# Weights traced two blocks ahead, and norms in a fixed TensorE order, in a two-block transformer kernel

## The chip, the cores and the metric

The kernel runs on one core of one Trainium2 chip. The metric is the device time of one execution in microseconds (us). The engines are named as in the profile: PE is TensorE (PEld its weight loads), DVE is VectorE, ACT is ScalarE, POOL is GpSimd, SP is SyncE, which issues the loads of the weights.

## The reference, cut to what matters

The input is 256 tokens of 1024 channels, in fp32. A first block has four layers of attention (differential, latent, dilated, differential) with a SwiGLU each, all with rms norms. The second block, cut to its core, is where most of the change lies; the dilated attention of the first block (layer C) is the other place.

```
def second_block(x, ...):
    h = layer_norm(x, ln_in_g, ln_in_b)
    for l in range(2):
        mix = token_mix(h, ...)
        h = layer_norm(DEEPNORM_ALPHA * h + mix, ln1_g[l], ln1_b[l])
        ffn = conv_ffn(h, w_up[l], ffn_dw_w[l], ffn_dw_b[l], w_down[l])
        h = layer_norm(DEEPNORM_ALPHA * h + ffn, ln2_g[l], ln2_b[l])
    return h

def token_mix(h, ...):
    z = h @ w_in + b_in
    u_pool, u_conv, q, k, v, qi, ki, wi, gates = split_cols(z, IN_SIZES)
    ...                                  # rope on q, k, qi, ki
    y_pool = pool_mixer(u_pool, pool_w, pool_scale) @ w_pool_out
    y_conv = conformer_conv(u_conv, ...) @ ...       # glu, 31 taps, layer norm, silu
    y_attn = dsa_attention(q, k, v, qi, ki, wi) @ w_attn_out
    g = jax.nn.sigmoid(gates).reshape(B, L, 3, D_MODEL)
    return (g[:, :, 0] * y_pool + g[:, :, 1] * y_conv + g[:, :, 2] * y_attn) @ w_o

def conv_ffn(h, w_up, ffn_dw_w, ffn_dw_b, w_down):
    u = causal_dwconv(h @ w_up, ffn_dw_w, ffn_dw_b)  # 3 taps
    gate, val = jnp.split(u, 2, axis=-1)
    return (jax.nn.silu(gate) * val) @ w_down
```

In `dsa_attention` an index score (8 heads, relu, weighted sum) selects the 64 best keys of each query, and the attention of 8 heads with 2 key heads runs over these.

## The kernel before

Activations lie transposed: `self.x[k]` is a chunk of 128 channels by 256 tokens, k from 0 to 7. Every large product is made of three (`mm3`): operands are split into a high and a low part, and high by high, high by low and low by high are summed in PSUM.

`weights` (L295) brings one block of weights: two pieces of up to 1024 columns; for each a load on SP's queue (L303), the high part `whi` by ScalarE (`act`, L236) and the low part `wlo` by VectorE (L308). There are five buffers for raw pieces and six for split ones, so three blocks of two pieces fit in the split buffers.

The order of each engine is written when the kernel is built: of the instructions that are ready, the one that comes first in the trace (the order in which the Python code makes them) goes first. Only where `self.woven` is set are products and transposes (`matmul` L264, `transpose` L318) held on TensorE in the order of the trace. In such stretches (layer C and `token_mix`) short steps are put between the products of the projections: `later(delay, step)` puts a step into a heap with a due time, `tick(us)` moves a planned clock forward by an estimate after each product, and due steps are traced then.

In `token_mix` the products of the projections come in this order: w_zqi (index queries), w_zb (keys, values), w_zq (queries), w_zs 0 (pool), w_zs 1 and 2 (glu of the convolution), then ten gate blocks (w_zs 5 to 14, j from 2 to 11 in the loop) with two blocks of convolution taps (w_tap) after j = 3 and j = 5. Woven in as steps are: `turn` (transposes of the roped qi and q), `keys`, `index` (one head of the index score), `greatest` (a round of the top-k on VectorE: two max and two replace operations), `roped`, `tapped` (three convolution taps on VectorE), `pooled`, and `attend`, `returned`, `mixed` (the attention). The rounds of the top-k are due 1.5 apart, the steps of attend 6.0 apart.

`deepnorm` adds a residual chunk by chunk as the products of a projection end; per chunk `seen` makes the square, sums x on VectorE and the square on GpSimd (`moments`, k 0 to 6 added, the last one left over), and splits x times the gain for early products. `entry` does the same at the start of the second block, with a third sum `st["x"]`. `normed` then calls `stats` (`compact` sums over channels with one-column matmuls against `onesd`, L1055; `spread` makes the scale and the shift on VectorE and GpSimd and broadcasts them by transposes, L319), makes the products of two weight blocks with the not yet normalised x (k 0 to 7, so the norm is applied to their results), and `ln_apply` normalises x itself for the blocks that follow. `self.woven` is not set there. The last norm has its own `last_norm`, which calls `compact` too.

Of the kernel before, what the change touches and what calls it, by code (L numbers as in the profile page):

```python
# [14 lines left out]
AF = mybir.ActivationFunctionType  # L15
# [196 lines left out]
class Program:  # L212
# [82 lines left out]
    def weights(self, ap, unit, eng=None):  # L295
# [52 lines left out]
    def mmode(self, aps, n, kb, xs):  # L348
        ps = [self.mm_bank()[:, :n] for _ in range(2)]
        for b, ap in enumerate(aps):  # L350
            w = self.ready.pop() if self.ready else self.weights(ap, n)
            kt = [(k, t) for k in range(kb) for t in range(2)]
            if b == len(aps) - 1:
                kt.sort(key=lambda a: a[1])
            for k, t in kt:
                kk = b * kb + k
                xh, xl = xs[kk]
                tk = slice(t * 128, t * 128 + 128)
                self.mm3(ps[t], (xh[:, tk], xl[:, tk]), w(k, 0, n),
                         b == 0 and k == 0, b == len(aps) - 1 and k == kb - 1)  # L360
                if self.woven:
                    self.tick(3 * US[n])
        return ps
# [191 lines left out]
    def project(self, w, xs, consume, late=None, eng=None):  # L555

        for j in range(4):
            wt = self.weights(w[j], 256, eng)
# [305 lines left out]
    def dilated(self, l, own):  # L864
# [18 lines left out]
        self.woven = True  # L883
        v, done = {}, [0]

        def values(hq):
            for g in range(3):
                v[hq // 2, g] = self.v_block([wv[g, hq], wv[g, hq + 1]], xs, r)

        def queries(hq):  # L890
# [4 lines left out]
            for g in (1, 2, 0):  # L895
                ps = self.mmode([wqk[g, hq][0], wqk[g, hq][1]], 512, 4, xs)
                toks = list(self.qk_tokens(ps, r, "ropeC", -0.125))
# [93 lines left out]
        for j in range(4):  # L991
            wt[j] = self.weights(self.ins["w_co"][j], 256)
# [44 lines left out]

    def moments(self, k, chunk, accs, eng):

        if k == 0:  # L1040
            accs.append(self.wk.tile([128, 256], F32, name="acc", tag="acc", bufs=3))
            eng.tensor_copy(accs[0], chunk)
        elif k < 7:
            eng.tensor_add(accs[0], accs[0], chunk)  # L1044
        else:
            accs.append(chunk)

    def compact(self, sums):
# [3 lines left out]
        for r in range(m):  # L1052
            for n, a in enumerate(sums):
                for t in range(2):
                    self.nc.tensor.matmul(ps[:, 2 * n + t:2 * n + t + 1], a[r][:, t * 128:(t + 1) * 128],  # L1055
                                          self.onesd[:, 0:1], start=r == 0 and n == 0 and t == 0,
                                          stop=r == m - 1 and n == len(sums) - 1 and t == 1,
                                          skip_group_check=True)
        return ps
# [11 lines left out]
    def spread(self, mean, sq, eps, extra=None):  # L1071
# [19 lines left out]
        self.stt(b, m, -1.0, r, OP.mult, OP.mult)  # L1091
        return self.bcast(r, b)

# [56 lines left out]
    def seen(self, st, k):  # L1150
        x = self.x[k]
        sq = self.t1("sq")
        self.act(sq, x, AF.Square)
        self.moments(k, x, st["m"], self.nc.vector)
        self.moments(k, sq, st["q"], self.nc.gpsimd)
        if st["early"]:
# [138 lines left out]
    def token_mix(self, l, st):  # L1295
# [21 lines left out]

        def by_token(w, o):

            bz = bias(o, 512)  # L1320
            ps = self.mmode([w[l, 0], w[l, 1]], 512, 4, xs)
            tok = [self.t2("qtok") for _ in range(2)]
# [12 lines left out]
        qiT = self.slot()  # L1335
        for t, q in enumerate(by_token(i["w_zqi"], 0)):
            self.rope(heads(q, 8), 8, 32, *tab[t])
# [3 lines left out]
        bz = bias(512, 328)  # L1341
        ps = self.mmode([i["w_zb"][l, 0], i["w_zb"][l, 1]], 328, 4, xs)
        kd = self.t2("zkd", (2, 256))
# [32 lines left out]
        def index(hh):  # L1376
# [11 lines left out]
            if hh == 7:  # L1388
# [25 lines left out]
        toks = by_token(i["w_zq"], 840)  # L1414

# [12 lines left out]
        w = self.weights(i["w_zs"][l, 0], 256)  # L1428
        u = wk.tile([128, 2, 256], F32, name="up", tag="pl", bufs=4)
# [23 lines left out]
        gp.tensor_sub(s1, s1, u)  # L1453
        cvp = self.cvp
        for f in range(2):
            w = self.weights(i["w_zs"][l, 1 + f], 256)
            ps = self.smode2(w, xs)
            th = self.t1("glu")
            self.act(th, ps[:, 1, :], AF.Tanh, scale=0.5, bias=self.hb[:, l, f:f + 1])
            nc.vector.tensor_scalar(th, th, 0.5, 0.5, op0=OP.mult, op1=OP.add)  # L1460
            self.stt(cvp[:, f, 30:286], ps[:, 0, :], self.col(f"bc{l}", f), th, OP.add, OP.mult)

        cv = [self.t1("cv") for _ in range(2)]
        taps = self.rslot().rearrange("p a b -> p (a b)")[:, :572].rearrange("p (s n) -> p s n", s=2)
        self.split(taps[:, 0, :], taps[:, 1, :], cvp[:, 1, :], 1.0)
        wcol = lambda t: self.col(f"cw{l}", t)
        self.act(cv[0], cvp[:, 0, 0:256], AF.Identity, scale=wcol(0), bias=self.col(f"cb{l}", 0))

        def tapped(t0):
            for t in range(t0, t0 + 3):  # L1470
                self.stt(cv[0], cvp[:, 0, t:t + 256], wcol(t), cv[0], OP.mult, OP.add)

        for n in range(10):
            self.later(6.0 + 4.0 * n, lambda n=n: tapped(1 + 3 * n))
        pp = [wk.tile([128, 2, 256], R, name=f"pp{f}", tag="pl", bufs=4) for f in range(2)]
# [8 lines left out]

        self.later(34.0, pooled)

# [42 lines left out]
        for c in range(4):  # L1529
            es = {}  # L1530
            for e in range(2):
                self.later(11.0 + 6.0 * (2 * c + e), lambda c=c, e=e, es=es: attend(c, e, es))


        gt += [self.slot() for _ in range(5)]
        for j in range(2, 12):
            w = self.weights(i["w_zs"][l, 3 + j], 256)
            ps = self.smode2(w, xs)
            for f in range(2):
                opened(2 * j + f, ps[:, f, :])  # L1540
            if j in (3, 5):
                b = (j - 3) // 2
                if b == 0:
                    tap = self.sc_bank()[:, :256]
                w = self.weights(i["w_tap"][l, b], 128)
                for k in range(16 - b):
# [14 lines left out]

        wpo = self.weights(i["w_po"][l], 1024)
        wco = self.weights(i["w_cvo"][l], 1024)
        part = []
# [9 lines left out]
        for hf in range(2):  # L1574
            w = self.weights(i["w_ato"][l, hf], 512)
            for ff in range(4):
# [8 lines left out]
        chunk, st = self.deepnorm(f"ln1_g{l}", f"ln1_b{l}", True)  # L1585
        self.project(i["w_2o"][l], ms, chunk)
        return st

    def conv_ffn(self, l, st, more):
# [7 lines left out]
        xs = self.normed(st, [up[l, j] for j in range(2)], first)  # L1597
        hs = self.split_slots(FC)
        for j in range(FC):
            if j < 2:  # L1600
                p = [ps0[j, f] for f in range(2)]
            else:
                ps = self.smode2(self.weights(up[l, j], 256), xs)
                p = [ps[:, f, :] for f in range(2)]
# [47 lines left out]
```

## Time and profile before

| what | value |
|---|---|
| median of 3 runs | 2310.9 us (2309.01 to 2315.43) |
| profiled execution: its time, its span | 2312.77 us, 2310.9 us |
| mean granted clock of TensorE | 0.986 |
| TensorE matmul busy | 2225.8 us, 96% |
| VectorE busy | 1629.7 us, 71% |
| ScalarE busy | 1325.3 us, 57% |
| GpSimd busy | 225.5 us, 10% |

The times of the trace are those of the profiled execution; its span runs from the first to the last instruction, and the execution's own time is 1.9 us longer. Layer C runs from 617 to 957 us, the first `token_mix` from 1442 to 1660, its norm and `conv_ffn` to 1879, the second `token_mix` from there to 2080, the second `conv_ffn` to 2298, and the last norm ends the span.

### The profile page before, as it was taken

The numbers are of one execution on the slowest core, as the hardware profiler recorded it, in microseconds if no ns is written. First come the engines' busy times: TensorE is split into PE (matmuls) and PEld (weight loads), VectorE is DVE, ScalarE is ACT, GpSimd is POOL, SyncE is SP. The second block draws the span as 40 slices with busy tenths as digits, with TensorE's granted clock in tenths as the row PEclk, the third lists the DMA queues.
The fourth block names the chain that finished last, engine by engine and source line by source line (L and its number), as shares of the span: only waits on it lengthen the run. The fifth ranks groups of instructions, "written<-read, shape, count | busy, mean of one in ns | idle before, by whom it ended". The sixth has DMA issues, their size and how long they took to land.

```text
span 2310.9 us, 42575 instructions
## 1 busy us (share of the span) xinstructions
PE 2225.8 (96%) x16624; PEld 2094.2 (91%) x16624; DVE 1629.7 (71%) x2924; ACT 1325.3 (57%) x2410; POOL 225.5 (10%) x231
## 2 busy tenths in 40 slices
PE   8999998999999999999999999989989998998998
PEld 6899997899977778999978999889989997998998
DVE  6776666776556656766577766796888678778875
ACT  7764456554456655644487545645566564556653
POOL 1010012300010000100101001110012011001211
PEclk9999999999999999999999999999999999999999
DMA  6345553354654344355633655544545544443643
GB/s 230 135 156 183 160 173 123 106 189 157 193 179 148 111 137 137 130 186 159 205 128 102 219 170 160 183 145 138 174 132 200 157 151 156 163 154 136 206 158 107
DMA packets 112569, 365.93 MB, mean 158 GB/s; under 512 B 12528, under 2 KB 15728, under 8 KB 112368
## 3 DMA queue, kind: packets, MB, share of 16 engines
q1 hardware_dynamic: 109968, 359.64, 47.4%
q10 hardware_dynamic: 2256, 3.31, 0.4%
q8 instruction: 131, 2.15, 0.4%
q14 instruction: 70, 0.57, 0.1%
q0 software_dynamic: 144, 0.26, 0.1%
HBM read 362.38 MB, written 1.05 MB: 157 GB/s over the span
## 4 chain that ended last, share of the span: by engine, by line
PE 61%; DVE 6%; ACT 3%; issue 1%; POOL 0%; DMA 0%; ACTq 0%; DVEq 0%; POOLq 0%
PE mm L265 53%; PE sc L265 5%; PE tp L319 2%; DVE wlo L308 1%; ACT whi L236 1%; DVE xl L239 1%; ACT xh L236 1%; ACT x L236 0%; PE tp L265 0%; DVE score L1401 0%; PE tp L1055 0%; PE tp L708 0%; DVE mx L1400 0%; DVE gut L239 0%; DVE acc L1044 0%
## 5 line engine op out<-in xcount | busy, mean ns | idle before, releaser
L308 DVE TENSOR_TENSOR wlo<-raw,whi 128x1024 fp32r<-128x1024 f32 (+2 forms) x744 | 840.5, 1134 | 357.7 <-ACT whi L236 354.5
L236 ACT ACTIVATE whi<-raw 128x1024 fp32r<-128x1024 f32 (+3 forms) x752 | 731.3, 978 | 574.8 <-PE mm L265 375.3
L265 PE MATMUL mm<-xh,wlo 128*128 128x256 f32 x2496 | 706.6, 283 | 20.0 <-DVE wlo L308 20.0
L265 PE MATMUL mm<-xh,whi 128*128 128x256 f32 x2496 | 713.0, 286 | 0.4 <-ACT whi L236 0.4
L265 PE MATMUL mm<-xl,whi 128*128 128x256 f32 x2496 | 705.7, 283 | 1.4 <-DVE xl L239 1.0
L265 PE MATMUL mm<-s,whi 128*128 128x256 f32 x2976 | 544.7, 284 | 0.0
L265 PEld LDWEIGHTS mm<-xh,wlo 128*128 128x128 f32 x2496 | 474.6, 190 | 21.1 <-DVE wlo L308 21.1
L265 PEld LDWEIGHTS mm<-xl,whi 128*128 128x128 f32 x2496 | 475.3, 190 | 3.2 <-DVE xl L239 1.7
L265 PEld LDWEIGHTS mm<-xh,whi 128*128 128x128 f32 x2496 | 475.5, 191 | 2.8 <-issue 1.0
L265 PEld LDWEIGHTS mm<-s,whi 128*128 128x128 f32 x2976 | 465.5, 192 | 5.0 <-issue 3.8
L265 PE MATMUL mm<-s,wlo 128*128 128x256 f32 x1488 | 421.2, 284 | 0.0
L265 PEld LDWEIGHTS mm<-s,wlo 128*128 128x128 f32 x1488 | 285.3, 192 | 0.1
L265 PE MATMUL mm<-whi,xh 128*128 128x512 f32 (+3 forms) x608 | 243.4, 401 | 14.8 <-ACT whi L236 10.0
L265 PE MATMUL mm<-wlo,xh 128*128 128x512 f32 (+3 forms) x608 | 239.7, 394 | 3.5 <-DVE wlo L308 3.5
L265 PE MATMUL mm<-whi,xl 128*128 128x512 f32 (+3 forms) x608 | 237.7, 391 | 0.0
L265 PEld LDWEIGHTS mm<-whi,xh 128*128 128x128 f32 x608 | 116.1, 191 | 38.0 <-ACT whi L236 10.4
L265 PEld LDWEIGHTS mm<-wlo,xh 128*128 128x128 f32 x608 | 116.2, 191 | 23.6 <-DVE wlo L308 4.8
L265 PEld LDWEIGHTS mm<-whi,xl 128*128 128x128 f32 x608 | 116.2, 191 | 22.3
L480 POOL TENSOR_TENSOR sqacc<-sqacc,sq 128x256 f32<-128x256 f32 x56 | 57.2, 1022 | 586.6 <-ACT sq L236 584.0
L236 ACT ACTIVATE s<-guh 128x256 fp32r<-128x256 f32 x132 | 54.9, 416 | 102.4 <-DVE guh L532 94.8
L528 DVE TENSOR_TENSOR gut<-mm,rbc 128x512 f32<-128x512 f32 x88 | 60.4, 690 | 39.9 <-PE mm L265 39.9
L236 ACT ACTIVATE s<-tp 128x512 fp32r<-128x512 f32 (+4 forms) x96 | 50.3, 524 | 62.1 <-PE tp L819 25.6
(316 smaller groups left out, 2532.6 us busy)
## 6 DMA issues: line engine op xcount, KB each, us to landing
raw<-w_gu SPq DMA_DIRECT2D x176, 512.0 KB, 4.5
raw<-w_up SPq DMA_DIRECT2D x88, 512.0 KB, 4.1
raw<-w_zs SPq DMA_DIRECT2D x60, 512.0 KB, 4.8
raw<-w_out SPq DMA_DIRECT2D x64, 384.0 KB, 3.2
raw<-w_cqk SPq DMA_DIRECT2D x48, 512.0 KB, 4.2
raw<-w_out SPq DMA_DIRECT2D x64, 320.0 KB, 2.8
raw<-w_aqk SPq DMA_DIRECT2D x32, 512.0 KB, 4.6
raw<-w_cv SPq DMA_DIRECT2D x24, 512.0 KB, 4.1
```

Source lines behind the costliest of these rows:

```text
L236: return self.nc.scalar.activation(out, in_, func, bias=bias, scale=scale, **kw)
L239: return self.nc.vector.scalar_tensor_tensor(out, a, s, b, op0=op0, op1=op1)
L265: i = self.nc.tensor.matmul(*a, **kw)
L308: e.tensor_sub(lo, raw, hi.bitcast(F32))
L319: i = self.nc.tensor.transpose(out, in_, self.ident if ident is None else ident)
L480: self.nc.gpsimd.tensor_add(acc, acc, sq)
L528: nc.vector.tensor_mul(t, ps, rb[:, None, :].to_broadcast([128, 2, 256]))
```

## The change

Four things are changed.

1. A new helper `feed(blocks, ahead)` takes the whole list of weight blocks of a stretch; at each call it traces the weights up to `ahead` blocks beyond the one that is handed out. Layer C and `token_mix` (ahead = 2) and the up projection of `conv_ffn` (from j = 2, ahead = 1) take their weights from it. Before, a block's weights were traced right before its products.
2. `normed` makes its weights and banks first, sets `self.woven`, and has the order: products k 0 to 3, `stats` with its sums, products 4 to 6, the broadcast transposes, product 7. `spread` now returns its two columns, and the broadcast is made in `normed`. `compact` makes its matmuls through `self.matmul`, so they are held in order there.
3. `moments` takes `apart`: where a norm has no third sum (`st["x"]` empty: ln1 and ln2 of each layer), only the chunks 0 to 3 are added on VectorE and GpSimd, and chunks 4 to 7 go into `compact` one by one. Such a norm has 2 x 2 x 5 = 20 calls there instead of 8, each of two passes (40 matmul instructions instead of 16); the entry norm keeps its 12 calls (24).
4. In `token_mix` the glu and its taps are moved ahead of the pool step, and due times are changed: rounds of the top-k from 1.5 to 2.3 apart, `attended` from 24 to 26, `pooled` from 34 to 44, `attend` from 11 + 6.0 n to 15 + 5.6 n.

```diff
+    def feed(self, blocks, ahead=2):
+        made, asked = [], [0]
+
+        def get():
+            while len(made) < len(blocks) and len(made) <= asked[0] + ahead:
+                made.append(self.weights(*blocks[len(made)]))
+            asked[0] += 1
+            return made[asked[0] - 1]
+
+        return get
...
-            w = self.ready.pop() if self.ready else self.weights(ap, n)
+            w = ap() if callable(ap) else self.ready.pop() if self.ready else self.weights(ap, n)
...
+        vals = lambda hq: [(wv[g, hq + n], 512) for g in range(3) for n in range(2)]
+        keyed = lambda *hqs: [(wqk[g, hq][n], 512) for hq in hqs for g in (1, 2, 0) for n in range(2)]
+        feed = self.feed(vals(0) + keyed(0, 1, 2) + vals(2) + keyed(3) + [(self.ins["w_co"][j], 256) for j in range(4)])
...
-        elif k < 7:
+        elif k < apart:
             eng.tensor_add(accs[0], accs[0], chunk)
...
-                    self.nc.tensor.matmul(ps[:, 2 * n + t:2 * n + t + 1], a[r][:, t * 128:(t + 1) * 128],
+                    self.matmul(ps[:, 2 * n + t:2 * n + t + 1], a[r][:, t * 128:(t + 1) * 128],
...
-        return self.bcast(r, b)
+        return r, b
...
+        apart = 7 if st["x"] else 4
+        self.moments(k, x, st["m"], self.nc.vector, apart)
+        self.moments(k, sq, st["q"], self.nc.gpsimd, apart)
...
     def normed(self, st, aps, take):
-        rb = self.stats(st)
+        self.woven = True
         ps = [[self.sc_bank(), self.sc_bank() if n == 0 else self.mm_bank()] for n in range(len(aps))]
         ws = [self.weights(ap, 256) for ap in aps]
-        for k in range(8):
-            for n, w in enumerate(ws):
-                for f in range(2):
-                    self.mm3(ps[n][f][:, :258], w(k, f * 128), st["z"][k], k == 0, k == 7)
+        def products(k0, k1):
+            for k in range(k0, k1):
+                for n, w in enumerate(ws):
+                    for f in range(2):
+                        self.mm3(ps[n][f][:, :258], w(k, f * 128), st["z"][k], k == 0, k == 7)
+        products(0, 4)
+        rb = self.stats(st)
+        products(4, 7)
+        rb = self.bcast(*rb)
+        products(7, 8)
+        self.woven = False
         xs = self.ln_apply(rb, st["g"], st["b"])
...
+        gates = [(i["w_zs"][l, 3 + j], 256) for j in range(2, 12)]
+        taps = [(i["w_tap"][l, n], 128) for n in range(2)]
+        feed = self.feed([(i[n][l, b], u) for n, u in (("w_zqi", 512), ("w_zb", 328), ("w_zq", 512)) for b in range(2)]
+                         + [(i["w_zs"][l, n], 256) for n in (1, 2, 0)]
+                         + gates[:2] + taps[:1] + gates[2:4] + taps[1:] + gates[4:]
+                         + [(i["w_po"][l], 1024), (i["w_cvo"][l], 1024)]
+                         + [(i["w_ato"][l, hf], 512) for hf in range(2)]
+                         + [(i["w_2o"][l, j], 256) for j in range(4)])
...
-                    self.later(1.5 * rd, lambda rd=rd: greatest(rd))
+                    self.later(2.3 * rd, lambda rd=rd: greatest(rd))
...
-        self.later(24.0, attended)
+        self.later(26.0, attended)
...
-        self.later(34.0, pooled)
+        self.later(44.0, pooled)
...
-                self.later(11.0 + 6.0 * (2 * c + e), lambda c=c, e=e, es=es: attend(c, e, es))
+                self.later(15.0 + 5.6 * (2 * c + e), lambda c=c, e=e, es=es: attend(c, e, es))
...
+        feed = self.feed([(up[l, j], 256) for j in range(2, FC)], 1)
```

## Rows read from the trace of the kernel before

**Rows 1.** The page, busy time of the engines over the span.

```profile
PE 2225.8 (96%) x16624; PEld 2094.2 (91%) x16624; DVE 1629.7 (71%) x2924; ACT 1325.3 (57%) x2410; POOL 225.5 (10%) x231
```

**Rows 2.** Waits of TensorE in total: who waits for whom; us, times, longest.

```profile
PE mm L265 <- DVE wlo L308: 23.5, 7, 6.3
...
PE tp L265 <- POOL sqacc L480: 2.1, 2, 1.1
```

**Rows 3.** Windows: length, busy time of five engines, granted clock, DMA share, GB/s.

```profile
1490.00:1493.40 3.40, 3.12 (x11) 3.12 (x12) 3.40 (x6) 1.10 (x2) 0.00 (x0) 0.50 0.55 201
1521.50:1539.40 17.90, 11.61 (x95) 10.97 (x93) 17.90 (x70) 6.08 (x10) 6.33 (x11) 0.95 0.00 1
1537.80:1544.60 6.80, 3.93 (x18) 3.93 (x19) 6.80 (x11) 0.81 (x2) 0.00 (x0) 0.50 0.41 133
1681.10:1687.90 6.80, 6.80 (x33) 6.80 (x33) 3.39 (x7) 0.05 (x1) 0.81 (x1) 0.50 0.24 80
```

**Rows 4.** Timeline of both mixes at the late gate block.

```profile
1518.39 1.05 ACT L236 ACTIVATE whi<-raw 128x1024 fp32r<-128x1024 f32 x1
...
1538.40 0.68 DVE L432 TENSOR_TENSOR qtok<-qtok,ropet 128x512 f32<-128x512 f32 x1
...
1539.40 1.21 DVE L308 TENSOR_TENSOR wlo<-raw,whi 128x1024 fp32r<-128x1024 f32 x1
...
1540.67 0.58 PE L265 MATMUL mm<-xh,wlo 128*128 128x256 f32 x1 [6.26 <-DVE wlo L308]
...
1545.12 0.60 PE L319 MATMUL tp<-pk,qtok 128*128 128x128 f32 x4
...
1959.20 0.58 PE L265 MATMUL mm<-xh,wlo 128*128 128x256 f32 x1 [6.25 <-DVE wlo L308]
```

**Rows 5.** The chain that ended last, one long stretch of products.

```profile
963.82 188.55 PE mm L265 x1536
```

**Rows 6.** Timeline of TensorE, entry norm and front of the first mix.

```profile
1458.77 1.40 PE L1055 MATMUL tp<-onesd,acc 128*128 128x1 f32 x12
...
1467.35 0.43 PE L319 MATMUL tp<-pk,lnr 128*128 128x128 f32 x2 [0.69 <-DVE lnr L1089]
1467.62 0.38 PE L319 MATMUL tp<-pk,lnb 128*128 128x128 f32 x2
...
1490.28 0.64 PE L265 MATMUL mm<-wlo,xh 128*128 128x328 f32 x1 [2.73 <-DVE wlo L308]
```

**Rows 7.** Timeline, ln2 and front of the second mix.

```profile
1879.35 0.95 PE L1055 MATMUL tp<-onesd,acc 128*128 128x1 f32 x8
...
1884.61 0.38 PE L319 MATMUL tp<-pk,lnb 128*128 128x128 f32 x2
...
1888.65 0.69 DVE L1105 TENSOR_TENSOR xl<-x,xh 128x512 fp32r<-128x512 f32 x1 [0.29 <-ACT x L236]
...
1899.96 0.50 PE L265 MATMUL mm<-whi,xh 128*128 128x512 f32 x1 [1.14 <-ACT whi L236]
1901.22 0.50 PE L265 MATMUL mm<-wlo,xh 128*128 128x512 f32 x1 [0.76 <-DVE wlo L308]
```

**Rows 8.** Timeline, first norm in front of conv_ffn and its block 4.

```profile
1675.34 0.28 PE L265 MATMUL sc<-xh,whi 128*128 128x258 f32 x1
...
1679.66 0.58 PE L1055 MATMUL tp<-onesd,acc 128*128 128x1 f32 x4 [2.71 <-DVE acc L1044]
...
1689.87 0.38 PE L319 MATMUL tp<-pk,lnb 128*128 128x128 f32 x2
...
1695.31 0.69 DVE L1105 TENSOR_TENSOR xl<-x,xh 128x512 fp32r<-128x512 f32 x1 [0.23 <-ACT x L236]
...
1711.32 0.39 PE L265 MATMUL mm<-xh,wlo 128*128 128x256 f32 x1 [3.14 <-DVE wlo L308]
```

**Rows 9.** Timeline of GpSimd, rms norm of layer C.

```profile
639.96 7.52 POOL L480 TENSOR_TENSOR sqacc<-sqacc,sq 128x256 f32<-128x256 f32 x6
```

**Rows 10.** Timeline of TensorE, sums of the last norm.

```profile
2298.40 0.95 PE L1055 MATMUL tp<-onesd,acc 128*128 128x1 f32 x8
```

More of the change, by code (lines that the diff above doesn't have):

```diff
@@ L557, in project @@
         for j in range(4):
-            wt = self.weights(w[j], 256, eng)
+            wt = w() if callable(w) else self.weights(w[j], 256, eng)
             if j < 3:
@@ L895, in queries @@
             for g in (1, 2, 0):
-                ps = self.mmode([wqk[g, hq][0], wqk[g, hq][1]], 512, 4, xs)
+                ps = self.mmode([feed, feed], 512, 4, xs)
                 toks = list(self.qk_tokens(ps, r, "ropeC", -0.125))
@@ L991, in dilated @@
         for j in range(4):
-            wt[j] = self.weights(self.ins["w_co"][j], 256)
+            wt[j] = feed()
             ps[j] = (self.mm_bank() if j < 3 else self.sc_bank()).rearrange("p (f n) -> p f n", f=2)
@@ L1032, in conv_norm, with moments @@
             self.act(v[k], v[k], AF.Silu, scale=self.col(g, k), bias=self.col(b, k))
-    def moments(self, k, chunk, accs, eng):
+    def moments(self, k, chunk, accs, eng, apart=7):
         if k == 0:
@@ L1054, in compact @@
                 for t in range(2):
-                    self.nc.tensor.matmul(ps[:, 2 * n + t:2 * n + t + 1], a[r][:, t * 128:(t + 1) * 128],
-                                          self.onesd[:, 0:1], start=r == 0 and n == 0 and t == 0,
-                                          stop=r == m - 1 and n == len(sums) - 1 and t == 1,
-                                          skip_group_check=True)
+                    self.matmul(ps[:, 2 * n + t:2 * n + t + 1], a[r][:, t * 128:(t + 1) * 128],
+                                self.onesd[:, 0:1], start=r == 0 and n == 0 and t == 0,
+                                stop=r == m - 1 and n == len(sums) - 1 and t == 1, skip_group_check=True)
         return ps
@@ L1316, in token_mix, with by_token @@
         self.woven = True
-        def by_token(w, o):
+        def by_token(o):
             bz = bias(o, 512)
-            ps = self.mmode([w[l, 0], w[l, 1]], 512, 4, xs)
+            ps = self.mmode([feed, feed], 512, 4, xs)
             tok = [self.t2("qtok") for _ in range(2)]
@@ L1335, in token_mix @@
         qiT = self.slot()
-        for t, q in enumerate(by_token(i["w_zqi"], 0)):
+        for t, q in enumerate(by_token(0)):
             self.rope(heads(q, 8), 8, 32, *tab[t])
@@ L1341, in token_mix @@
         bz = bias(512, 328)
-        ps = self.mmode([i["w_zb"][l, 0], i["w_zb"][l, 1]], 328, 4, xs)
+        ps = self.mmode([feed, feed], 328, 4, xs)
         kd = self.t2("zkd", (2, 256))
@@ L1409, in token_mix @@
             self.later(11.2 + 1.3 * hh, lambda hh=hh: index(hh))
-        self.later(24.0, attended)
+        self.later(26.0, attended)
         qT = self.slot()
-        toks = by_token(i["w_zq"], 840)
+        toks = by_token(840)
         def roped(t):
@@ L1427, in token_mix, with tapped @@
             nc.gpsimd.tensor_copy(self.bd[rows, g // 2, rows], pwv[rows, g // 2, :])
-        w = self.weights(i["w_zs"][l, 0], 256)
+        cvp = self.cvp
+        for f in range(2):
+            ps = self.smode2(feed(), xs)
+            th = self.t1("glu")
+            self.act(th, ps[:, 1, :], AF.Tanh, scale=0.5, bias=self.hb[:, l, f:f + 1])
+            nc.vector.tensor_scalar(th, th, 0.5, 0.5, op0=OP.mult, op1=OP.add)
+            self.stt(cvp[:, f, 30:286], ps[:, 0, :], self.col(f"bc{l}", f), th, OP.add, OP.mult)
+        cv = [self.t1("cv") for _ in range(2)]
+        taps = self.rslot().rearrange("p a b -> p (a b)")[:, :572].rearrange("p (s n) -> p s n", s=2)
+        self.split(taps[:, 0, :], taps[:, 1, :], cvp[:, 1, :], 1.0)
+        wcol = lambda t: self.col(f"cw{l}", t)
+        self.act(cv[0], cvp[:, 0, 0:256], AF.Identity, scale=wcol(0), bias=self.col(f"cb{l}", 0))
+        def tapped(t0):
+            for t in range(t0, t0 + 3):
+                self.stt(cv[0], cvp[:, 0, t:t + 256], wcol(t), cv[0], OP.mult, OP.add)
+        for n in range(10):
+            self.later(6.0 + 4.0 * n, lambda n=n: tapped(1 + 3 * n))
+        w = feed()
         u = wk.tile([128, 2, 256], F32, name="up", tag="pl", bufs=4)
@@ L1453, in token_mix @@
         gp.tensor_sub(s1, s1, u)
[L1454 to L1474, printed above, removed]
         pp = [wk.tile([128, 2, 256], R, name=f"pp{f}", tag="pl", bufs=4) for f in range(2)]
@@ L1531, in token_mix @@
             for e in range(2):
-                self.later(11.0 + 6.0 * (2 * c + e), lambda c=c, e=e, es=es: attend(c, e, es))
+                self.later(15.0 + 5.6 * (2 * c + e), lambda c=c, e=e, es=es: attend(c, e, es))
         gt += [self.slot() for _ in range(5)]
         for j in range(2, 12):
-            w = self.weights(i["w_zs"][l, 3 + j], 256)
-            ps = self.smode2(w, xs)
+            ps = self.smode2(feed(), xs)
             for f in range(2):
@@ L1544, in token_mix @@
                     tap = self.sc_bank()[:, :256]
-                w = self.weights(i["w_tap"][l, b], 128)
+                w = feed()
                 for k in range(16 - b):
@@ L1560, in token_mix @@
             self.split(ch[f], cl[f], cv[f], 1.0)
-        wpo = self.weights(i["w_po"][l], 1024)
-        wco = self.weights(i["w_cvo"][l], 1024)
+        wpo, wco = feed(), feed()
         part = []
@@ L1574, in token_mix @@
         for hf in range(2):
-            w = self.weights(i["w_ato"][l, hf], 512)
+            w = feed()
             for ff in range(4):
@@ L1585, in token_mix @@
         chunk, st = self.deepnorm(f"ln1_g{l}", f"ln1_b{l}", True)
-        self.project(i["w_2o"][l], ms, chunk)
+        self.project(feed, ms, chunk)
         return st
@@ L1602, in conv_ffn @@
             else:
-                ps = self.smode2(self.weights(up[l, j], 256), xs)
+                ps = self.smode2(feed(), xs)
                 p = [ps[:, f, :] for f in range(2)]
```

4 lines of the change are left out of this document (1 added, 3 removed).

## The prediction, made before the changed kernel had run

> **What bounds the kernel now.** I read the page first: TensorE is busy for 96% of the span [rows 1], so only two things can move the time, TensorE's own instructions and the few places where it stands still. The waits of TensorE name those places: 23.5 us in seven waits for a wlo, the low half of a split weight piece, which VectorE makes, and 2.1 us in two waits for the sum of squares of an rms norm [rows 2]. The windows then show that a long wait is paid twice. Behind the waits that end at 1490.3, 1540.7 and 1679.7 the granted clock was 0.50, which is 1.2 of the two levels 1.2 and 2.4 GHz, for 3.4, 6.8 and 6.8 us [rows 3]; half of such a stretch is lost, 1.7 or 3.4 us. The same windows say why the wlo is late: VectorE was busy for 17.90 of 17.90 us ahead of 1539.4 [rows 3]. Last I read the timeline there. The high half of the piece was begun at 1518.39 and done 1.05 later; its wlo began at 1539.40, twenty microseconds on, behind index rounds and ropes that stand earlier in the trace; TensorE had waited 6.26 us [rows 4]. The second layer has the same wait, 6.25 [rows 4]. So one such place costs 6.3 + 3.4 = 9.7 us, and there are two.
>
> **The change, part by part.** The pitch of a 256-column product is 188.55 / 1536 = 0.123 us over a long stretch of the chain [rows 5]; I take 0.120 for the unbroken runs of the norms, so a step k of `normed` (two weights, two halves, three products) costs 12 x 0.120 = 1.44 us. A one-column sum matmul has 1.40 us for 12 and 0.95 for 8 [rows 6, 7], so 0.45 / 4 = 0.1125 us each. Sums of norms without `st["x"]` go from 16 to 40 such matmuls, so each gains 24 x 0.1125 = 2.7 us of TensorE's time, in place of VectorE and GpSimd additions. The Trainium skill, TensorE: Matmul & The Clock Gate, section Back-to-back issue gap, lists a floor of about 25 ns for so few columns; by it the 24 would be 0.6 us and each norm 2.1 us cheaper. The rows decide.
>
> *Interior of the two mixes.* Weights of gate blocks are traced before the index rounds, so four wlo (blocks 2 and 3, two pieces each) of 1.21 us [rows 4] go ahead of ropes and rounds on VectorE. The 9.7 us go. But VectorE has no free time there, so 4 x 1.21 = 4.84 us of other work slides, and the glu moved ahead of the pool step brings its taps forward too. What is late next are the transposes of q: the rope of its second half ended at 1538.40 + 0.68, and TensorE took it up at 1545.12 only because it had stood for the wlo [rows 4]; the first half was taken up with no slack. These transposes are pinned, so every later product is queued behind them. I take 4.0 of the 4.84 as a new wait there, a half-clock stretch of the short kind behind it (1.7), and 1.5 for the returns of attend, which now stand behind earlier taps. Respacing the index steps from 1.5 to 2.3 spreads the rounds but takes none away; pooled at 44 keeps its own wait, since its second matmul waits on its first's eviction either way. Net -9.7 + 4.0 + 1.7 + 1.5 = -2.5 each, -5.0 for two. Bounds: -9.7 (nothing late in its place) and +4 (all 4.84 waited, the long half clock, and returns 3 late, together 11.2, plus a weight block that still comes late, 2.5).
>
> *Front of the first mix (entry norm, 24 sums before and after).* The wait for w_zb's wlo, 2.73 us, whose VectorE turn came after ropes [rows 6], goes, with 1.7 of half clock [rows 3]: -4.4. Against it the order is pinned: from 1458.77, products 0 to 3 (5.76), sums (2.7), products 4 to 6 (4.32) and the broadcast (0.44) end at 1472.0, where before it ended at 1467.62 + 0.38 = 1468.0 [rows 6]. Only product 7 (1.44) is left to cover `ln_apply`, which took 1888.65 + 0.69 - 1884.99 = 4.35 us from the broadcast to the first xl [rows 7]. So the next product starts at 1476.3; before it followed the products at 1458.77 + 8 x 1.44 + 2.7 + 0.44 + 0.69 (a wait) = 1474.1 [rows 6]. Loss 2.2, net -2.2.
>
> *The two norms in front of conv_ffn.* Before, sums came first, 2.71 us were waited for an accumulator and 3.4 lost at half clock behind it [rows 3, 8]. After, from the end of the project at 1675.34, where its first product stands now: 5.76 + 4.5 (40 sums) + 4.32 + 0.44 gives 1690.4, against 1689.87 + 0.38 before [rows 8]: no gain at the broadcast. What can be gained lies behind it: the first xl was done at 1695.31 + 0.69 [rows 8], 5.75 after the broadcast with weight splits in between, where ln2 took 4.35 [rows 7], 1.4 less; the splits are traced ahead now. I take half of that, -0.7 each, -1.4 in all; the wait for block 4's wlo of 3.14 [rows 8] stays, since that piece is behind the same ScalarE chain and one block ahead changes nothing there. Bounds -1.4 and +1.7 each (a new half clock).
>
> *ln2 in front of the second mix.* From 1879.35: 5.76 + 4.5 + 4.32 + 0.44 the broadcast ends at 1894.4, and xl 4.35 later, 1898.7. Before, products ended at 1879.35 + 11.52 + 1.8 (16 sums) + 0.44 = 1893.1 with xl long there (1889.3) [rows 7]. Loss 5.6; the weights come early now, which takes away the waits of 1.14 and 0.76 [rows 7] and leaves 3.7; products that need xh alone start a little sooner: +3.5. Bounds 2 and 7 (with a long half clock).
>
> *Layer C.* Splits two blocks ahead put two whi (1.05 us each [rows 4]) before the Squares of the rms, whose sum on GpSimd runs 7.52 us for six additions [rows 9]; TensorE waits for that sum already, 1.1 us at most [rows 2], so it is late by 0 to 2.1: +1.5. The other waits of the layer that I read are not for weights; bounds -1 and +3 for the layer.
>
> *Last norm.* Nothing is left to hide 24 more sums behind the last product at 2298.40 [rows 10]; the removed additions had long ended: +2.7. *Feed in conv_ffn*: no product of its steady blocks waits for weights, so 0.
>
> Sum: -5.0 - 2.2 - 1.4 + 3.5 + 1.5 + 2.7 = -0.9 us on the profiled execution's 2312.8, so 2311.9; the median of the runs lies 1.9 under that execution, so 2310.0.
>
> **Rivals.** *Nothing takes the stalls' place.* Spaced rounds leave gaps in which the ropes go, and both mixes give back 9.7: -19.4 in place of -5.0, so 2295.6. For it: rounds at 2.3 leave others more room between them than at 1.5. Against it: VectorE was full for 17.90 us [rows 3], and work that slides is waited for by a pinned instruction. *The norms' order is wrong for TensorE.* With products spent before the sums, `ln_apply` lies open four times. If VectorE's and ScalarE's weight splits, traced ahead of it now, go in between as they did in ln1 (5.75 from broadcast to xl instead of 4.35 [rows 8]) and each open wait of over 2.7 brings a half clock of 1.7 to 3.4, the four norms cost 1.4 + 2.5 more each, 15.6 in all: 2326. It decides where the open wait is as long as the 2.71 us that had a half clock behind it [rows 3, 8]. *The sums themselves cost the clock.* A run of 40 one-column matmuls, 4.5 us, has no like here; the longest run in a norm was 12 [rows 6]. If the clock halves behind it in the three norms with 40 sums and pinned products, 3.4 each, about 10 us: 2320. The Trainium skill, same page, section A second HAM failure mode: psum-queue depth-cycling, tells of a clock that falls by short idle spells between groups; by that rule this rival comes true. No run of such matmuls in this trace shows it or denies it. *The change does nothing that counts*: the splits are bound by ScalarE and by buffers coming free, not by their place in the trace, so stalls move by a block: 2311, inside the forecast's band.
>
> **How the numbers follow.** Forecast with the do-nothing rival: 0.39 (of which 0.10 is the latter). Stalls gone: 0.26, and a half-way case, where one mix gains fully or both gain about 5, at 2302, 0.09. Norm order: 0.17. Clock behind the sums: 0.09. A measurement here can tell about 0.3%, 6.9 us, from no change. So faster 0.35, same 0.39, slower 0.26. The likeliest case gives 2310, with 2304 to 2317 as its own range. The whole range reaches down to the gone stalls with a little from ln1, 2294, and up to most of the norm rival, 2324.
>
> **What would show it.** In the profile after: the waits of TensorE for wlo fall from 23.5 to under 8, and new rows name qtok, aT or xl; in ln1, ln2 and the entry a wait of 2 to 5 us for xh or xl sits in front of the first product that uses them; the 40 one-column matmuls of a norm stand in one run behind its first 48 products, and the tail is 2.7 longer. The forecast is wrong if VectorE is no longer full ahead of the gate blocks and no row with qtok has over 1 us (then the stalls are gone), or if the granted clock is 0.50 behind the sums of a norm with no wait in front (then the sums cost the clock).

## The result, and the profile after

The changed kernel takes 2330.1 us (median of 5 runs, 2324.3 to 2333.7), the kernel before 2311.1: a ratio of 1.0077, with a 95% interval of 1.0057 to 1.0097. The forecast was 2310 with a range to 2324; the change made the kernel slower, and by more than the range allowed. The profiled execution has a span of 2328.3 us against 2310.9.

TensorE's busy time on the page after, to be set beside [rows 1], is 17.7 us longer, and its instructions are 96 more: 24 more sums in each of four norms.

```profile
PE 2243.5 (96%) x16720; PEld 2108.3 (91%) x16720; DVE 1621.9 (70%) x2912; ACT 1323.8 (57%) x2410; POOL 218.4 (9%) x219
```

The waits of TensorE after (who waits for whom; us in all, times, longest) answer to [rows 2]:

```profile
PE tp L332 <- DVE qtok L445: 7.3, 5, 2.5
PE mm L265 <- DVE xl L1120: 6.3, 4, 1.7
PE tp L265 <- POOL sqacc L493: 6.3, 2, 4.0
...
PE mm L265 <- DVE s L239: 4.3, 6, 1.2
...
PE mm L265 <- ACT xh L236: 4.1, 4, 1.3
PE mm L265 <- DVE zt L1383: 3.1, 2, 1.7
...
PE mm L265 <- DVE wlo L308: 2.0, 2, 1.2
```

The 23.5 us of waits for wlo are down to 2.0, as forecast. Nothing is won by it: waits for qtok (1.9 before), xl, xh, zt and for s (the splits of the gated sums, in front of the mixes' last projection) have come or grown, and that for the sum of squares went from 2.1 to 6.3, 3.0 of it in layer C.

To see where the time went, I read off the timeline when the first sum or product of each norm began. After:

```profile
454.05 0.39 PE L265 MATMUL tp<-ones,sqacc 128*128 128x1 f32 x3
...
963.44 0.28 PE L265 MATMUL tp<-ones,sqacc 128*128 128x1 f32 x2
...
1464.99 0.28 PE L265 MATMUL sc<-xh,whi 128*128 128x258 f32 x1
...
1682.94 0.28 PE L265 MATMUL sc<-xh,whi 128*128 128x258 f32 x1
...
1889.79 0.28 PE L265 MATMUL sc<-xh,whi 128*128 128x258 f32 x1
...
2109.83 0.28 PE L265 MATMUL sc<-xh,whi 128*128 128x258 f32 x1
...
2312.73 0.28 PE L265 MATMUL tp<-onesd,acc 128*128 128x1 f32 x2
```

With the same instants of before ([rows 6, 7, 8, 10] have four of them; the other three are 451.45, 957.32 and 2094.45) the stretches are these, in us:

| stretch | before | after | difference | forecast |
|---|---|---|---|---|
| start to the rms norm in front of the second ffn (same code) | 451.4 | 454.0 | +2.6 | 0 |
| to the rms norm behind layer C | 505.9 | 509.4 | +3.5 | +1.5 |
| to the entry norm | 501.5 | 501.6 | +0.1 | 0 |
| entry norm and first mix | 216.6 | 217.9 | +1.4 | -4.7 |
| ln1 and conv_ffn | 204.0 | 206.9 | +2.8 | -0.7 |
| ln2 and second mix | 215.1 | 220.0 | +4.9 | +1.0 |
| ln1 and conv_ffn | 204.0 | 202.9 | -1.1 | -0.7 |
| last norm | 12.5 | 15.6 | +3.1 | +2.7 |

The first row is the same program in both kernels; so much differs from one execution to the next (over the thirteen profiled executions of this document the stretch ends between 449.95 and 454.38). The others show that no stretch of a norm or a mix gained more than 1.1 us.

The windows of ln1 (first layer), ln2 and ln1 (second layer) show something that [rows 3] had not. The columns are those of [rows 3]; 1688.90 to 1693.30 is the run of 40 sums of the first ln1, and the second line is what follows it. The third line begins inside the run of ln2, which starts at 1895.56, and the fourth with the last sums of the second ln1. The fifth is at the waits for xh and xl in the first ln1.

```profile
1688.90:1693.30 4.40, 4.40 (x42) 4.40 (x41) 1.99 (x2) 1.40 (x2) 0.00 (x0) 1.00 0.83 260
1693.30:1696.70 3.40, 3.40 (x17) 3.40 (x17) 1.70 (x5) 0.00 (x0) 0.70 (x1) 0.50 0.51 184
...
1898.10:1904.90 6.80, 6.80 (x33) 6.80 (x33) 1.70 (x5) 0.00 (x0) 0.70 (x1) 0.50 0.26 75
...
2119.90:2123.30 3.40, 3.40 (x17) 3.40 (x18) 1.70 (x5) 0.00 (x0) 0.70 (x1) 0.51 0.47 171
...
1703.50:1710.30 6.80, 6.01 (x28) 6.01 (x29) 5.82 (x11) 5.25 (x15) 0.00 (x0) 0.50 0.44 154
```

In the second to fourth lines TensorE is busy for all of 3.40 and 6.80 us by the profile, has waited for nothing, and yet the granted clock is 0.50. In [rows 3] each half-clock stretch had a wait in front of it.

The fifth line, and a stretch of 3.4 us at 0.50 from 1727.4, have no like in the second ln1 and conv_ffn, though the waits for xh, xl and gut there are the same to 0.1 us. This is most of what sets the 206.9 us of the first apart from the 202.9 of the second.

Last, the first mix in the timeline after (the idle time and what ended it is in brackets):

```profile
1482.57 0.50 PE L265 MATMUL mm<-whi,xh 128*128 128x512 f32 x1 [1.26 <-ACT xh L236]
...
1484.77 0.56 PE L265 MATMUL mm<-whi,xl 128*128 128x512 f32 x1 [1.47 <-DVE xl L1120]
...
1503.52 3.49 DVE L308 TENSOR_TENSOR wlo<-raw,whi 128x1024 fp32r<-128x1024 f32 x3
1506.92 0.49 DVE L1383 TENSOR_TENSOR zt<-mm,bz 128x328 f32<-128x328 f32 x1
...
1507.47 0.51 PE L265 MATMUL mm<-whi,xh 128*128 128x512 f32 x1 [1.46 <-DVE zt L1383]
...
1541.29 0.66 PE L332 MATMUL tp<-pk,qtok 128*128 128x128 f32 x4 [1.05 <-DVE qtok L445]
...
1548.40 0.41 PE L332 MATMUL tp<-pk,qtok 128*128 128x128 f32 x2 [2.54 <-DVE qtok L445]
...
1648.15 0.50 PE L265 MATMUL mm<-s,whi 128*128 128x256 f32 x2 [0.22 <-DVE s L239]
...
1651.09 0.50 PE L265 MATMUL mm<-s,whi 128*128 128x256 f32 x2 [1.25 <-DVE s L239]
...
1657.81 0.39 PE L265 MATMUL mm<-s,whi 128*128 128x256 f32 x1 [0.70 <-DVE s L239]
```

Where [rows 4] had one wait of 6.26, there are now 1.46 for zt, 1.05 and 2.54 for qtok, and 2.17 in three pieces in front of the last projection; in front of them 1.26 and 1.47 for the normalised x.

### The profile page after: what moved, and what is told of

It reads as the page before. It is cut to its first block, busy times and chain, and to the rows that moved or that the text cites. A ratio compares the mean times of both kernels' runs of the same rounds, so it can differ in the third digit from the quotient of the medians.

```text
span 2328.3 us, 42761 instructions
## 1 busy us (share of the span) xinstructions
PE 2243.5 (96%) x16720; PEld 2108.3 (91%) x16720; DVE 1621.9 (70%) x2912; ACT 1323.8 (57%) x2410; POOL 218.4 (9%) x219
## 3 DMA queue, kind: packets, MB, share of 16 engines
HBM read 362.38 MB, written 1.05 MB: 156 GB/s over the span
## 4 chain that ended last, share of the span: by engine, by line
PE 61%; DVE 5%; ACT 3%; issue 1%; DMA 1%; POOL 0%; DVEq 0%; ACTq 0%; SPq 0%; POOLq 0%
PE mm L265 52%; PE sc L265 5%; PE tp L332 2%; DVE wlo L308 2%; PE tp L265 1%; ACT whi L236 1%; PE tp L721 0%; DMA raw<-w_zs 0%; DVE score L1435 0%; ACT s L236 0%; ACT xh L236 0%; DVE mx L1434 0%; ACT gut L236 0%; DVE xl L239 0%; DVE gut L239 0%
```

## The experiments

Each run is compared with runs of the kernel before on the same chip, and ratios are to that kernel; the changed kernel stands at 1.0077. A thousandth is 2.3 us.

**1. The added sums undone.**

```diff
-        apart = 7 if st["x"] else 4
+        apart = 7
```

> The changed kernel with all four norms adding seven chunks on VectorE and GpSimd again (16 sum matmuls a norm in place of 40), everything else kept. Theory A, the 24 extra sums of each norm are TensorE time that nothing hides: the stretches of the norms and the tail get shorter by 4 x 2.7 us, so about 2319 from 2330, and no wait for an accumulator comes back, since products 0 to 3 stand ahead of the sums. Rival B, the additions are as late as the sums were long: a wait for acc of 2 to 3 us stands in front of the sums, and the time stays within 3 us of 2330.

Measured: 2310.1 us, ratio 0.9991 (0.9981 to 1.0001): 20 us faster than the changed kernel, by one line, and about the time of the kernel before. Theory A was right in kind and half the size. No wait for acc came back. The windows of this run's ln1, the 16 sums and what follows them:

```profile
1685.90:1687.80 1.90, 1.90 (x19) 1.90 (x19) 1.90 (x3) 1.82 (x2) 0.00 (x0) 1.00 0.13 30
1687.80:1691.20 3.40, 3.40 (x30) 3.40 (x30) 3.40 (x6) 0.00 (x0) 0.00 (x0) 1.00 0.90 261
```

The clock holds at 1.00 behind 16 sums. So the 40 cost more than themselves (4 x 2.7 would be 10.8 us).

**2. The order of the norms undone, with the 40 sums.**

```diff
-        self.woven = True
+        rb = self.bcast(*self.stats(st))
         ps = [[self.sc_bank(), ...
-        products(0, 4)
-        rb = self.stats(st)
-        products(4, 7)
-        rb = self.bcast(*rb)
-        products(7, 8)
-        self.woven = False
+        products(0, 8)
```

> The changed kernel with the order of the norms of before (sums first, then all products, not pinned), the 40 sums kept. Theory A, the pinned order opens ln_apply: the waits for xh and xl behind product 7 (2.5 to 2.7 us in each of four norms) go, and about 8 us come back, 2322. Rival B, what the order opens behind the products it saves in front of the sums: a wait for the last chunk's square stands there instead and the time stays at 2330 within 3. Rival C, the half clock of 3.4 us behind each run of sums comes from the run being in one piece: spread between the products it is gone, 1.7 us a norm.

Measured: 2318.5 us, ratio 1.0032 (1.0020 to 1.0043), 10 to 12 us faster than the changed kernel. The waits for xh and xl of the blocks behind the norms are gone, as theory A has it. Rival C's remark on the clock was not tested: left free, the scheduler still put the first 20, 32 and 20 of the 40 sums of the three norms in one run (in the first ln1 from 1672.32 to 1674.57) and the rest in groups of 4 and 8 between products, and the clock is halved in all three. The first:

```profile
1675.20:1685.40 10.20, 10.20 (x50) 10.20 (x49) 4.32 (x10) 1.87 (x4) 0.34 (x1) 0.50 0.32 104
```

Of the 12 us between the two profiled executions, 4.1 stand in front of layer C's norm, in code that is the same.

**3. Layer C's weights right before their products.**

```diff
-        ... + keyed(3) + [(self.ins["w_co"][j], 256) for j in range(4)])
+        ... + keyed(3) + [(self.ins["w_co"][j], 256) for j in range(4)], 0)
```

> The changed kernel with the weights of layer C traced right before their products again. Theory A, the splits two blocks ahead stand in front of the squares of the rms: the wait for the sum of squares falls from 4.0 to 1.0 us, the half clock behind it is shorter, and layer C is 3.5 us shorter, 2326.5. Rival B, layer C's difference is one of the granted clock from run to run: the wait falls but the time stays within 1.5 us.

Measured: 2325.4 us, ratio 1.0053 (1.0040 to 1.0066). The interval overlaps that of the changed kernel, so the times alone don't settle it; the traces do. Layer C's waits in this run:

```profile
PE mm L265 <- ACT s L236: 3.3, 1, 3.3
...
PE tp L265 <- POOL sqacc L493: 1.0, 1, 1.0
```

The wait for the sum of squares is 1.0 again, against 4.0 in the changed kernel (its longest in the table of waits above), and the stretch of layer C is 505.1 us against 509.4 and 505.9. The next wait, for s, is 3.3 again, where the changed kernel had 1.2, so the two waits together are only 0.9 apart; most of the rest goes with the granted clock, 0.50 for 13.7 us of the layer there and for 6.8 here. Over all traces of this document the stretch takes 507.3 to 509.4 us in the five kernels with two blocks ahead in layer C and 505.0 to 505.9 in the eight without: theory A.

**4. The mixes' weights right before their products.**

```diff
-                         + [(i["w_2o"][l, j], 256) for j in range(4)])
+                         + [(i["w_2o"][l, j], 256) for j in range(4)], 0)
```

> The changed kernel with the weights of both mixes and of their last projection traced right before their products again; the moved glu and the new due times are kept. Theory A, the feed only moves the waits: a wait for wlo of some 6 us comes back in front of a gate block in each mix, and the waits for zt (1.5), qtok (1.1 and 2.5), aexp (1.2) and for the split of the gated sums (2.2) go, so 2330 within 4. Rival B, the feed is what the change gains, and the due times and the pinned norms are what it loses: waits come back and none goes, 2342 or more. Rival C, the feed is a loss even in the mixes: 2324 or less.

Measured: 2321.7 us, ratio 1.0041 (1.0027 to 1.0054). That is rival C by direction, a loss of the feed in the mixes, with some 8 us where 6 or more were asked. The waits of the first mix in this run:

```profile
PE mm L265 <- DVE wlo L308: 4.5, 2, 3.6
PE sc L265 <- DVE pp L239: 2.2, 1, 2.2
PE mm L265 <- DVE xl L1120: 1.5, 1, 1.5
PE mm L265 <- ACT xh L236: 1.3, 1, 1.3
```

The waits for zt, qtok, aexp and s are gone, and the wait for wlo that comes back is 3.6 and 0.9, not 6.3.

**5. All three undone: seven chunks added, layer C and the mixes without feed.** The edits of runs 1, 3 and 4 together.

> The changed kernel with three parts undone at once: seven chunks added on VectorE and GpSimd in all norms, and the weights of layer C and of both mixes traced right before their products. Left of the change are the pinned order of the norms, the glu ahead of the pool step with the new due times, and one block ahead in conv_ffn. Theory A, the parts act in their own stretches and add: -20 of the sums, -4.7 of layer C, -8.4 of the mixes, so 2297, under the kernel before. Rival B, the mixes' gain in the run with 40 sums came from the granted clock there and is not had a second time: 2304 or more.

Measured: 2295.9 us against 2313.7 of the kernel before, ratio 0.9928 (0.9914 to 0.9942). Theory A holds: the parts add. This version beats both kernels, the one before by 17.8 us and the changed one by some 34.

**6. As run 5, with the order of the norms undone too.** The edits of runs 2 and 5.

> As the run with these three parts undone, and the norms in the order of before too: sums first, not pinned. Left are the moved glu, the new due times and one block ahead in conv_ffn. Theory A, the pinned order opens ln_apply (waits for xh and xl of 2.0 to 2.7 us a norm) and gives up less in front of the sums: 2 to 6 us faster than that run, 2293. Rival B, with 16 sums the order of before brings back its waits for the accumulator (2.7 us and a half clock, twice) and for late wlo pieces: 3 to 8 us slower than that run, 2302. Against the kernel before it shows what the glu and the due times do alone: a wait of 3.7 and 0.9 in place of 6.3, 0.9 and 0.5 in each mix, 2 to 4 us a mix.

Measured: 2304.1 us, ratio 0.9959 (0.9945 to 0.9973). Rival B: with 16 sums the pinned order is worth 8 us. And what is left here, the moved glu and the new due times (with one block ahead in conv_ffn), is worth 9.6 us against the kernel before.

**7. As run 5, with the mixes one block ahead.**

```diff
+                         + [(i["w_2o"][l, j], 256) for j in range(4)], 1)
```

> As the run with the three parts undone, but the mixes' weights one block ahead. Theory A, splits that come earlier only push the work that pinned instructions wait for: waits for zt, qtok and the gated sums come back in part, 2 to 8 us slower than that run, 2299 to 2305. Rival B, two blocks are too much and one is right: the wait of 3.7 for wlo goes and nothing comes for it, 3 to 8 us faster, 2290.

Measured: 2299.1 us, ratio 0.9937 (0.9924 to 0.9950). The interval overlaps that of run 5, and the two mixes together take 422.5 us in its trace against 422.4: no difference was shown. The wait for wlo became 1.53 and 0.50, and waits for qtok (1.24) and aexp (0.96) came, so waits come back in part, as theory A says, for no more than they replace.

**8. The 40 sums kept, but spread between the products.**

```diff
-        products(0, 4)
-        rb = self.stats(st)
+        if st["x"]:
+            products(0, 4)
+            rb = self.stats(st)
+        else:
+            rb = self.stats(st, products)
...
     def compact(self, sums, between=None):
         for r in range(m):
+            if between and r < 4:
+                between(r, r + 1)
```

> The changed kernel with the 40 sum matmuls of ln1 and ln2 put between products 0 to 3 in four portions (8, 8, 8 and 16) instead of one run behind them; the number of sums is kept, the tail too. Theory A, it is the run in one piece (4.4 us of one-column matmuls) that the granted clock answers to: the half clock behind the sums of the three norms goes, 1.7 to 3.4 us each, 2322. Rival B, the half clock comes whenever so many sums fall into a few us, or from something else there: it stays, 2330 within 3.

Measured: 2319.8 us against 2313.7, ratio 1.0031 (1.0020 to 1.0042): 10 us faster than the changed kernel with the same instructions. The windows of ln1, sums and products together, and what follows:

```profile
1676.90:1688.00 11.10, 11.10 (x96) 10.94 (x95) 7.38 (x15) 5.89 (x11) 0.00 (x0) 1.00 0.42 143
1688.00:1691.40 3.40, 3.40 (x30) 3.40 (x30) 2.17 (x5) 0.00 (x0) 0.71 (x1) 1.00 0.46 155
```

The clock is 1.00 there and behind the sums of all three norms. The last norm, whose 40 sums this run leaves in one piece from 2298.78 on, has the clock fall within them:

```profile
2301.00:2304.40 3.40, 3.40 (x18) 3.40 (x17) 0.00 (x0) 0.00 (x0) 0.00 (x0) 0.50 0.00 0
```

Theory A: it is the run in one piece. Of the 11.8 us between the two profiled executions 7.9 lie in the stretches of the three norms (4.2, 3.4 and 0.3) and 4.5 ahead of the entry norm, where the two kernels are the same; the last norm took 17.8 us where the changed kernel had 15.6.

**9. The 40 sums alone, in the kernel before.** The lines of `moments` and `seen` from the diff, nothing else.

> The kernel before with the 40 sums of the four norms without a third sum, and nothing else of the change. Theory A, the sums cost their own 2.7 us a norm, 10.8, and the granted clock falls behind them where they run nearly in one piece: 11 to 20 us slower, 2322 to 2331. Rival B, without the pinned order the scheduler puts products between the sums, the clock holds, and the wait for the accumulator (2.7 us, twice) goes as well: 6 us slower at most, 2317.

Measured: 2322.7 us against 2314.2, ratio 1.0038 (1.0024 to 1.0051), 8.5 us slower. Both theories have a part: the wait for acc is gone (5.4 us in two), and the clock falls. The windows of its first ln1, with the first 20 sums in one run and the others in groups between products, and what follows:

```profile
1675.68:1678.00 2.32, 2.32 (x23) 2.26 (x21) 2.32 (x6) 1.42 (x4) 0.00 (x0) 1.00 0.00 0
1678.00:1684.80 6.80, 6.80 (x34) 6.80 (x34) 3.40 (x7) 2.46 (x6) 0.00 (x0) 0.50 0.47 157
1684.80:1691.60 6.80, 6.80 (x33) 6.80 (x34) 1.68 (x5) 0.21 (x1) 0.70 (x1) 0.50 0.21 77
```

**10. The pinned order alone, in the kernel before, with its 16 sums.** `normed`, the return of `spread` and `self.matmul` in `compact` from the diff, nothing else.

> The kernel before with the pinned order of the norms (weights first, products 0 to 3, sums, products 4 to 6, broadcast, product 7) and 16 sums as before, and nothing else of the change. Theory A, the order takes away the waits for the accumulator and the half clock behind each, for more than the waits for xh and xl that it opens: 8 us faster, as between the two runs without feed, 2303. Rival B, the order pays only with the new due times in the mixes: within 3 us of 2311.

Measured: 2305.9 us against 2314.2, ratio 0.9966 (0.9953 to 0.9979), 8 us faster: theory A. Both stretches of ln1 and conv_ffn are 199.1 us, against 204.0 in the kernel before. The windows of its first ln1:

```profile
1674.10:1685.00 10.90, 10.90 (x93) 10.73 (x92) 10.90 (x20) 5.90 (x11) 2.35 (x3) 1.00 0.25 75
1685.00:1691.50 6.50, 3.96 (x30) 3.32 (x28) 5.10 (x9) 3.80 (x10) 0.70 (x1) 1.00 0.88 284
```

and all waits of over 0.6 us from there to ln2:

```profile
PE mm L265 <- DVE gut L239: 2.2, 1, 2.2
PE mm L265 <- DVE xl L1105: 1.7, 1, 1.7
PE mm L265 <- ACT xh L236: 0.8, 1, 0.8
```

There is no wait for acc and none for wlo (block 4's 3.14 of [rows 8] is gone, with 2.2 for gut in its place). The clock is 1.00, here even across the 2.5 us for xh and xl (0.8 and 1.7); at the same two waits in the changed kernel's first ln1 it was 0.50.

**11. The feed of the mixes alone, in the kernel before, with its old due times.** `feed` and its calls in `token_mix` from the diff, with the pool step still ahead of the glu.

> The kernel before with the weights of both mixes two blocks ahead, the order of the blocks and all due times as before, and nothing else of the change. Theory A, the waits move: the 6.3 us for wlo goes in each mix, and waits for zt, qtok, aexp and the gated sums come, of 8 us or more in all: 2311 to 2320. Rival B, the loss came from the new due times, which crowd the steps against the early splits: with the old ones the 6.3 us are won, 2300 or less.

Measured: 2320.8 us against 2314.2, ratio 1.0032 (1.0019 to 1.0045), 6.6 us slower: theory A. Waits that the first mix has got:

```profile
PE tp L332 <- DVE qtok L445: 4.4, 1, 4.4
PE tp L332 <- DVE zkd L1389: 2.6, 2, 1.9
PE mm L265 <- DVE s L239: 2.2, 3, 1.2
PE mm L265 <- DVE zt L1370: 2.1, 1, 2.1
```

## Why the prediction was wrong

**The sums.** Their own price was right: 40 matmuls from 1688.93 to the next product at 1693.34 are 0.110 us each, where the forecast had 0.1125 and the page of the Trainium skill that it cited (TensorE: Matmul & The Clock Gate, section Back-to-back issue gap) a floor of 0.025. The measurement decides.

```profile
1688.93 0.95 PE L265 MATMUL tp<-onesd,acc 128*128 128x1 f32 x8
...
1692.86 0.62 PE L265 MATMUL tp<-onesd,sq 128*128 128x1 f32 x4
1693.34 0.56 PE L265 MATMUL sc<-xh,whi 128*128 128x258 f32 x1
```

What failed is that the clock behind them was left out of the sum and put among the rivals, at a chance of 0.09. It is what happened: in the changed kernel and in runs 3 and 4 the granted clock was 0.50 in or behind each of the nine runs of 40 sums that have products behind them, in runs 1, 5, 7 and 10 behind none of the twelve runs of 16, and in run 8 behind none of the three norms with 40 sums in portions. The price of that rival was about right too: it put 10 us on it, and run 8 gives 10 back. By itself it gives 2320, inside the range. What the table has above the forecast elsewhere, 6.1 in the first mix with its norm, 2.0 in layer C and 2.6 in the code that is the same, brought the time over the upper end. The rival's condition was misread in one place: the longest run in a norm before was not 12 sums but the 16 of the last norm, from 2298.40 on, which has no product behind it. The Trainium skill, same page, section A second HAM failure mode: psum-queue depth-cycling, has the clock fall by short idle spells of TensorE between groups of matmuls. The rival came true, but these windows do not show that cause: TensorE is busy there for 3.40 of 3.40 us. Idle spells too short for the profile, in which the ends of matmuls are modelled, remain possible.

**Two cures for one wait.** The forecast let the 40 sums and the pinned order share the gain in ln1. Run 10 shows that the order takes away the wait for acc (2.7 us, and the half clock of [rows 3] behind it) by itself, and run 9 that the sums do so too, at a loss. Together the wait is taken away once and the sums are paid in full: undoing them brings 20 us in the changed kernel, while adding them costs 8.5 in the kernel before; and the order, worth 8 us with 16 sums, costs 10 to 12 with 40 (run 2). Of the 11.5 between 20 and 8.5, 5.4 are the two waits for acc; the rest, with the half clock behind these waits, was not split further. The term for ln1 was -0.7 each; the order alone is -4.9 each, and with the sums, their half clock and, in the first, the two other half-clock stretches it became +2.8 and -1.1. The term also let block 4's wait of 3.14 for a wlo stay. It is 2.7 in run 2, with one block ahead and the old order, and gone in run 10, with the pinned order and no block ahead: the order takes it away.

**The mixes.** The step "Net -9.7 + 4.0 + 1.7 + 1.5" failed on both sides. The gain was too large: of the half-clock stretch in [rows 3] TensorE was busy for 3.93 of 6.80 us, since the rest lies in the wait itself, so by this count the clock cost 2.0 and not 3.4, and the place 8.3. The row said so. And the price was too small: qtok and aexp took 4.7 (1.05, 2.54 and 1.15) where 5.5 were put, but two waits were not named at all, 1.46 for zt (a product of w_zq waits for the bank that VectorE has not read yet, since early splits stand in front of it) and 2.17 for the splits of the gated sums, in front of which now stand the splits of w_2o. Waits in the first mix were 12.9 us before and 13.3 after. The rule in it was right, that VectorE is full and what is put ahead of it makes something else late. Run 11 has the feed alone at +2.4 and +2.5 a mix by its stretches: inside the bound of +4, and on the other side of zero from the -2.5 taken. The due times and the moved glu, which the forecast gave no gain, are worth 9.6 us by run 6. Both together, with the 40 sums undone (run 1), the two stretches with a mix are 215.0 and 212.4 us, 1.6 and 2.7 under the kernel before. So the net of -2.5 was not far off there, but by luck: a loss that it had as a gain, and a gain that it had as nothing.

**Front of the mix and ln2.** The first xl was forecast for 1476.3, that is 1482.5 with the 6.2 us of delay that stand in front; the product that needs xh began at 1482.57, the one that needs xl at 1484.77, 2.2 late. Run 10 has the first mix at 216.7 us with this order, against 216.6: a gain of 2.2 was forecast, none was had. ln2 and the second mix are 214.1 there against 215.1, where the forecast had +3.5, 2.7 of it for the sums: there the order was priced 1.8 too dear.

**Layer C, the last norm and conv_ffn.** Layer C's step was right in kind and small in size: the wait for the sum of squares grew by 3.0, where 0 to 2.1 had been given, and the stretch by 3.5 for 1.5. The last norm's 2.7 measured 3.1. One block ahead in conv_ffn did nothing, as forecast: its stretches are 200.1 and 199.0 us in run 5 and 199.1 twice in run 10, which has none of it.

By single parts, the order (-8.3) and the due times with the glu (-9.6) are gains; the feed in the mixes (+6.6 to +8.4), that in layer C (4.7 between medians, with overlapping intervals) and the sums (+20 beside the order) are losses. They sum to between +13 and +15 against 19.0 measured; what remains is not assigned, and executions of the changed kernel alone differ by 9.

## What to carry to other kernels

Where an engine is full for tens of microseconds, tracing its work earlier can move a wait instead of removing it, as in both mixes here: list which pinned instructions wait for what is pushed back, the readers of PSUM banks among them. When two edits cure the same wait, price them together, since the second one pays its cost and gains nothing. And a half-clock stretch costs half of TensorE's busy time in it, not half of its length; the window's own column has the number (17 products in 3.40 us at 0.50 behind the sums, 30 in 3.40 us at 1.00 in run 1). Many one-column matmuls in one run are worth spreading between products: run 8 had 10 us from that with the same instructions.

## What the runs showed of the hardware

The granted clock of TensorE fell to 0.50 with no idle time that the profile shows: 3.40 of 3.40 and 6.80 of 6.80 us busy, in or behind 40 one-column matmuls in one run. In run 8 it stayed at 1.00 behind the 40 that stood between products and fell within the 40 that stood in one run. Runs 2 and 9 had it at 0.50 with 20 or 32 of the sums in one run and the others in groups of 4 and 8 behind them.

The clock does not answer alike in every execution. After the entry norm, whose 24 sums are one run as well, it fell in the changed kernel (0.50 from 1474.8) and not in run 1, with the same instructions there. At the two waits of 0.8 and 1.7 us for xh and xl, close together, it was 0.50 for 6.8 us in the changed kernel's first ln1, and 1.00 in its second and in both of run 10.
